# Table transfers behind the first MLP, first operands of the second MLP tile by tile, and one block sum on VectorE: a change in three parts to a two-layer trunk

## The chip, the cores and the metric

The kernel runs on one core of a Trainium2 chip. The metric is the time of one execution on the device in microseconds; a version's time is the median of its runs. A core has five engines, each with its own queue of instructions, which it works off in order: PE (matrix products), DVE (elementwise work on vectors), ACT (activations and copies), POOL (here only transfers, among them those that add to what stands at the target) and SP (here only transfers). Transfers are carried out by 16 DMA engines, which serve the queues of SP and POOL alike.

## The reference

512 tokens of width 1024 pass two layers. Layer 0 mixes by attention, layer 1 by a short gated convolution; after each mixer comes an MLP with a causal convolution of width 3 between its up projection and its gate. All is float32.

```python
def conv_ffn(h, norm_g, w_up, conv_w, w_down):
    xn = rms_norm(h, norm_g)
    u = causal_dwconv(xn @ w_up, conv_w)            # w_up: 1024 x 5632
    g, val = u[..., :D_FF], u[..., D_FF:]           # D_FF = 2816
    return (jax.nn.silu(g) * val) @ w_down

for layer in range(2):
    mixer = attention_mixer if layer % 2 == 0 else short_conv_mixer
    h = h + mixer(h, ...)
    h = h + conv_ffn(h, ffn_norm[layer], ffn_w_up[layer], ffn_conv[layer], ffn_w_down[layer])
```

## The kernel before

Every float32 product is made of three products of rounded halves: an operand is split into `hi` (a rounded copy, made by ACT, named `whi`, `p_hi`, `q_hi`) and `lo` (the rest, made by DVE from the operand and its `hi`, named `wlo`, `p_lo`, `q_lo`), and PE multiplies hi by hi, lo by hi and hi by lo. The helper `halves_to` (L1027, L1029) does this for the operands of the products below, L315 and L316 do it for the weights of the other products. In the trace PE's wait for a weight is therefore a wait for ACT's `whi` or, some 1.2 us later, for DVE's `wlo`.

The up projections go by groups of 256 columns of `w_up` (11 in each MLP, 0 to 10), and each group, but for the first two of the first MLP, by seven products of half-size blocks instead of eight (a Strassen-like scheme, class `Sevens`). The products, in PE's order, are p1, p7, p6, p2, q5, q4 and p3. Each has 24 matmuls (L1078), a form of the activations (made once, before group 0, from blocks a, b, c, d of the normed h; class `RawForms` in the second MLP) and a form of the weights (made for each group). The weights' blocks come into tiles X, Y, Z, W, three and four: some straight from `w_up`, some from tables in DRAM that hold sums of two or three blocks of `w_up`. Where a sum is not in a table, POOL adds a block by an accumulating transfer (`add_block`, L1105). In the second MLP q4's weights are `three` + W, and the sum is made in place in `three`, by such a transfer from `w_up`, after p6's `wlo` has read `three`; the reader of the sum is `whi_q` (`whi_q<-three` in the trace).

The tables (`t` in the trace) are built by POOL's transfers while other work runs (`table_steps`, L104 to L118): a step copies a block or a table (L117) or adds a block (L114), 1 MB or 768 KB each, and a step that builds on another waits for it. Those of the second MLP are 24 steps: 8 before the first MLP (`FAR`), 9 in the first MLP's up loop, one after every seventh slot, and 7 in the conv mixer. POOL takes its queue in order, so a step that waits also holds what stands behind it.

The down projection of an MLP (`mlp()`, L1675) follows after the last group. Its weights X_chain, Y_chain, p_hi_chain and so on (block sums again, the `_chain` tiles are loaded by SP at L291, and POOL adds to them at L289) and `raw` come 512 KB at a time. Where PE goes from the up to the down projection, the last group's products and the first weights of the down projection are wanted at the same time; that place is called the boundary. In the conv mixer, weights come as `raw` for its plain products and as Xc, Yc, Zc and Wc for its seven-product part; POOL adds to Yc at L1105.

The order on an engine is set by a scheduler with estimated times, and within stretches by the program's own order: between the last output tile of the conv mixer's output projection (o == 7) and slot 6 of the second MLP's group 0 the flag `strict` pins ACT and DVE to program order (those instructions have line L74 in the trace). In that stretch, the rest of h arrives, the norm's sum ends in a column `ncol_n` that PE spreads (L396) and ACT copies to `nrow_n`, and the forms p6, p2, q5, q4 of the activations are finished. `Norm.finish(EARLY, LATER)` gives the due times of the spread. s0 and s1 are scratch tiles in which forms that are differences are made.

Of the kernel before, what the change touches and what calls it, by code (L numbers as in the profile page):

```python
# [17 lines left out]
F32 = mybir.dt.float32  # L18
# [4 lines left out]
ALU = mybir.AluOpType  # L23
# [24 lines left out]
FILL1, FILL2, BEFORE = 1.5, 3.3, 2.0  # L48
UNITS = (0, 1), (2,), (3,)
PLAIN = 2, 0  # L50
FAR = 8
CHUNKS = ((2, 3), (5, 3), (8, 3)), ((0, 3), (3, 4), (7, 4))
EARLY, LATER = 4.0, 4.0
SHARE = 0.58


# [1 line left out]
def trunk(  # L58
# [1024 lines left out]
    class Sevens:  # L1083
# [74 lines left out]
        def slot(self, g, s):  # L1158

            on, was, soon = (i in self.groups for i in (g, g - 1, g + 1))  # L1160
            if self.chores:
                self.work_off(self.rate(g, s))
            form, n, fresh = (("p1", "A", True), ("p7", "T", True), ("p3", "R", False), ("p6", "R", False), ("p2", "A", False),
                              ("q5", "R", False), ("q4", "T", False))[s]
            if s == 2:
                if was:
                    self.product(g - 1, form, n, fresh)
            elif on:
                self.product(g, form, n, fresh)
            st, p, c = self.st, g - 1, self.st.get(g)  # L1170
            if s == 0:
                if was:
                    if "p3" not in st[p]:
                        self.weights_of(p, "p3", "Z")
                    self.join(p, "yg", st[p]["T"], st[p]["Xs"])
                if on:
                    self.load_one(g, "W", self.block_of(g, 1, 0))
                if soon:
                    self.load_pair(g + 1)
            elif s == 1:  # L1180
                first = not was
                if on and first and not self.ahead and "p6" not in c:
                    self.weights_of(g, "p6", "three" if self.table else "Y")
                if on:
                    act.activation(self.bank_of(g, "R"), c["A"], AF.Copy, scale=-1.0)
                if on and not first:
                    self.weights_of(g, "p6", "three" if self.table else "Y")
                if soon and not self.table:
                    self.add_block(g + 1, "Y", 1, 1)
            elif s == 2:  # L1190
                if on:
                    self.kept(g, "P7s", c["T"])
                    if "p2" not in c:
                        self.weights_of(g, "p2", "W")
                    if self.fours:
                        self.load_one(g, "four", self.table("4", g))
                    else:
                        c["four"] = c["three" if self.table else "Y"]
                        if self.scaled:
                            self.add_block(g, "four", 1, 0)  # L1200
                        else:
                            dve.tensor_tensor(c["four"], c["four"], c["W"], op=ALU.add)
            elif s == 3:
                if was:
                    self.early(p, st[p]["R"])
# [88 lines left out]
    class RawForms:  # L1294
# [1 line left out]


        def __init__(self, up, x, s0, s1):
            self.up, self.x, self.s = up, x, {"s0": s0, "s1": s1}

        def take(self, f):
            act.activation(self.x[f // 4][:, f % 4, :], h[:, f, :], AF.Copy, scale=gain_of(self.up.norm.base, f))

        def make(self, name, k=slice(0, 4)):
            (a, b), (c, d) = ((x[:, k, LEFT], x[:, k, RIGHT]) for x in self.x)
            s = {n: t() [:, k, :] if callable(t) else t[:, k, :] for n, t in self.s.items() if n == ("s1" if name == "q5" else "s0")}
            src, made = {
                "p1": (a, None), "p7": (s.get("s0"), (a, b, ALU.subtract)), "p6": (s.get("s0"), (s.get("s0"), d, ALU.add)), "p2": (c, None),
                "q5": (s.get("s1"), (b, d, ALU.subtract)), "q4": (d, None), "p3": (s.get("s0"), (c, s.get("s0"), ALU.subtract))}[name]
# [202 lines left out]
    def mlp(layer, norm, mp, begun_up=None):  # L1512
# [63 lines left out]
        n_up = 7 * (HF - PLAIN[layer])  # L1576
        for i, fn in enumerate(slots[:n_up]):
            fn()
            if layer == 0 and i % 7 == 6:
                sum_far(1)  # L1580
            left = n_up - i
            if left <= 2:
                operand(2 - left)
                fetch(3 - left)
# [118 lines left out]
                    finish(b)  # L1703
        if after_:
            after_.finish()
        return after_

    with tc.tile_pool(name="mlp0", bufs=1, reuse_waits="tile") as mp:
# [6 lines left out]
    with tc.tile_pool(name="mlp1", bufs=1, reuse_waits="tile") as mp:  # L1715
        norm = Norm("n3", 8)
        blocks, up = up_begin(1, norm, mp, rp)
        s0 = mp.tile([P, 4, HT], F32, tag="s0", name="s0_up")
        fresh = []

        def s1():
            if not fresh:
                fresh.append(hsp.tile([P, 4, HT], F32, tag="hs_b", name="s1_up"))
            return fresh[0]
        raw = RawForms(up, (place(4, 4), place(8, 4)), s0, s1)

        def out_products(w, acc, ks):
# [4 lines left out]
        def residual_out(o, acc):  # L1732
            dve.tensor_tensor(h[:, o, :], acc, h[:, o, :], op=ALU.add)
            raw.take(o)
            if o == ND - 1:
                raw.make("p6", slice(2, 4))
            norm.squares(o, h[:, o, :])

        first_two = [(weights(AHEAD - o), bank("ab"[o])) for o in range(2)]
# [7 lines left out]
        for o in range(2, ND):  # L1747
# [16 lines left out]

        def slot(g, s):
            up.slot(g, s)
# [29 lines left out]
```

## Time and profile before

| | |
|---|---|
| median of 3 runs | 1134.41 us (1133.47 to 1135.1) |
| the profiled execution | 1134.63 us, span 1132.9 us |
| busy | PE 1115.0, PEld 1016.2, DVE 957.7, ACT 679.8, POOL 175.9 us |
| DMA | 221.42 MB, mean 195 GB/s |
| POOL's queue | 43.4% of 16 engines' span, SP's 34.2% |

The profile counts times from the span's start. The first MLP runs from about 280 to 616 us, with its boundary at 495 to 516; the conv mixer to about 787; the second MLP from there, with its boundary at 1003 to 1016. POOL runs ahead: its last addition for the first MLP is issued at 563.74. A row of a timeline gives the start, the duration, the engine, the line, the operation, the written tile, `<-` and the read ones, and in brackets the idle time of the engine before it with the instruction that ended this. A row of windows gives the busy time of PE, PEld, DVE, ACT and POOL (with the number of instructions), then the granted clock of PE (1.00 is full), the DMA engines' busy share and GB/s. A row of waits gives who waited for whom: total us, times, longest. A row of the chain gives start, duration and what ran.

### The profile page before, as it was taken

How to read it: one execution, taken by the hardware profiler on the slowest of the kernel's cores; microseconds unless marked ns; L12 is line 12 of the kernel's file. 1: busy time of each engine (PE TensorE's matmuls, PEld its weight loads, DVE VectorE, ACT ScalarE, POOL GpSimd, SP SyncE). 2: the span in 40 equal slices, each digit the busy share in tenths (PEclk: the TensorE clock that was granted, in tenths of full speed). 3: DMA queues.
4: the chain of work that ended last, by engine and by line, in shares of the span. 5: the costliest groups of instructions: out<-in, count | busy, mean ns of one | idle time of the engine just before them, and what ended most of it. 6: DMA issues, size and time to landing. Idle time of an engine off the chain costs nothing.

```text
span 1132.9 us, 19709 instructions
## 1 busy us (share of the span) xinstructions
PE 1115.0 (98%) x7803; PEld 1016.2 (90%) x7803; DVE 957.7 (85%) x1471; ACT 679.8 (60%) x999; POOL 175.9 (16%) x204
## 2 busy tenths in 40 slices
PE   9999999999999999989999999999899999989998
PEld 7888787878899999989999899988899999988886
DVE  6798888988898787869989889856899999979886
ACT  7556677655567666656557345545656666557553
POOL 4011011111111120104300001001112121113300
PEclk9999999999999999999999999999999999989999
DMA  6678677777988899899953456697679797799961
GB/s 193 168 179 205 157 196 188 184 208 200 236 205 228 241 251 255 241 320 222 226 166 93 129 133 142 140 273 208 146 189 215 178 218 187 198 286 168 235 156 56
DMA packets 180540, 221.42 MB, mean 195 GB/s; under 512 B 7804, under 2 KB 144044, under 8 KB 180448
## 3 DMA queue, kind: packets, MB, share of 16 engines
q0 software_dynamic: 48912, 97.96, 43.4%
q1 hardware_dynamic: 131376, 122.14, 34.2%
q8 instruction: 61, 1.00, 0.3%
q14 instruction: 31, 0.25, 0.1%
q10 hardware_dynamic: 160, 0.07, 0.0%
HBM read 215.16 MB, written 53.48 MB: 237 GB/s over the span
## 4 chain that ended last, share of the span: by engine, by line
PE 90%; DVE 4%; DMA 3%; ACT 1%; issue 1%; SPq 0%; DVEq 0%; ACTq 0%
PE psb L1078 28%; PE psb L1675 11%; PE psa L1078 10%; PE psa L1675 8%; PE psb L336 6%; PE psb L338 5%; PE psb L337 5%; PE psb L710 2%; PE psa L338 2%; PE psa L337 2%; PE psa L336 2%; PE psa L807 2%; DMA four<-t 1%; DMA three<-in_ffn_w_up 1%; PE psc L782 1%; DMA X_chain<-in_ffn_w_down 1%
## 5 line engine op out<-in xcount | busy, mean ns | idle before, releaser
L1078 PE MATMUL psb<-p_hi,wlo_p 128*128 128x256 f32 x480 | 135.0, 282 | 1.5 <-DVE wlo_p L74 1.5
L1078 PE MATMUL psb<-p_hi,whi_p 128*128 128x256 f32 x480 | 135.1, 282 | 0.0
L1078 PE MATMUL psb<-p_lo,whi_p 128*128 128x256 f32 x480 | 135.1, 282 | 0.0
L315 ACT ACTIVATE whi<-raw 128x1024 fp32r<-128x1024 f32 (+2 forms) x81 | 83.2, 1028 | 81.8 <-PE psb L337 28.0
L316 DVE TENSOR_TENSOR wlo<-raw,whi 128x1024 fp32r<-128x1024 f32 (+2 forms) x81 | 95.7, 1182 | 24.7 <-ACT whi L315 24.1
L1078 PE MATMUL psb<-q_hi,whi_q 128*128 128x256 f32 x320 | 91.1, 285 | 2.7 <-ACT whi_q L1027 2.7
L1078 PE MATMUL psb<-q_hi,wlo_q 128*128 128x256 f32 x320 | 91.5, 286 | 1.9 <-DVE wlo_q L1029 1.9
L1078 PEld LDWEIGHTS psb<-p_hi,wlo_p 128*128 128x128 f32 x480 | 90.1, 188 | 1.7 <-DVE wlo_p L74 1.7
L1078 PE MATMUL psb<-q_lo,whi_q 128*128 128x256 f32 x320 | 91.1, 285 | 0.0
L1078 PEld LDWEIGHTS psb<-p_hi,whi_p 128*128 128x128 f32 x480 | 91.0, 190 | 0.0
L1078 PEld LDWEIGHTS psb<-p_lo,whi_p 128*128 128x128 f32 x480 | 90.4, 188 | 0.0
L1078 PE MATMUL psa<-p_hi,wlo_p 128*128 128x256 f32 x320 | 90.3, 282 | 0.0
L1078 PE MATMUL psa<-p_lo,whi_p 128*128 128x256 f32 x320 | 90.1, 282 | 0.0
L1078 PE MATMUL psa<-p_hi,whi_p 128*128 128x256 f32 x320 | 89.9, 281 | 0.0
L336 PE MATMUL psb<-hs_a,whi 128*128 128x512 f32 x192 | 79.4, 413 | 0.0
L338 PE MATMUL psb<-hs_a,wlo 128*128 128x512 f32 x192 | 76.2, 398 | 0.0
L1078 PEld LDWEIGHTS psb<-q_hi,whi_q 128*128 128x128 f32 x320 | 61.6, 193 | 3.2 <-ACT whi_q L1027 3.1
L1078 PEld LDWEIGHTS psb<-q_hi,wlo_q 128*128 128x128 f32 x320 | 61.2, 191 | 2.6 <-DVE wlo_q L1029 2.6
L1675 PE MATMUL psb<-act,whi 128*128 128x256 f32 x352 | 63.0, 282 | 0.1
L1078 PEld LDWEIGHTS psb<-q_lo,whi_q 128*128 128x128 f32 x320 | 61.3, 191 | 0.0
L1078 PEld LDWEIGHTS psa<-p_hi,whi_p 128*128 128x128 f32 x320 | 60.6, 190 | 0.1
L1078 PEld LDWEIGHTS psa<-p_hi,wlo_p 128*128 128x128 f32 x320 | 60.1, 188 | 0.2 <-DVE wlo_p L1029 0.2
(548 smaller groups left out, 3597.6 us busy)
## 6 DMA issues: line engine op xcount, KB each, us to landing
t<-in_ffn_w_up POOLq DMA_DIRECT2D x30, 768.0 KB, 8.0
raw<-in_attn_w_in SPq DMA_DIRECT2D x24, 512.0 KB, 5.2
t<-in_ffn_w_up POOLq DMA_DIRECT2D x12, 1024.0 KB, 12.6
t<-t POOLq DMA_DIRECT2D x14, 768.0 KB, 4.6
X<-in_ffn_w_up SPq DMA_DIRECT2D x20, 512.0 KB, 5.1
Y<-t SPq DMA_DIRECT2D x20, 512.0 KB, 6.6
three<-t SPq DMA_DIRECT2D x20, 512.0 KB, 5.7
W<-in_ffn_w_up SPq DMA_DIRECT2D x20, 512.0 KB, 4.0
```

Source lines behind the costliest of these rows:

```text
L315: return (act.activation(hi[:, at_], raw[:, at_], AF.Copy), dve.tensor_tensor(lo[:, at_], raw[:, at_], f32(hi[:, at_]), op=ALU.subtract))
L316: dve.tensor_tensor(lo[:, at_], raw[:, at_], f32(hi[:, at_]), op=ALU.subtract))
L336: made = [pe.matmul(acc, w[0], rhs[0], start=first, stop=False), pe.matmul(acc, w[0], rhs[1], start=False, stop=False), pe.matmul(acc, w[1 ...
L337: pe.matmul(acc, w[0], rhs[1], start=False, stop=False),
L338: pe.matmul(acc, w[1], rhs[0], start=False, stop=last)]
L710: pe.matmul(ss[e][:, c:c + wide], ql[rows, b * P:n], kl[rows, 0:wide], start=first and b == bs[0], stop=last and b == bs[-1])
L782: pe.transpose(t[:, k * P:(k + 1) * P], w[:, e, k * P:(k + 1) * P], ident)
L807: pe.matmul(out_, w, t[:, first:first + step * (NB - k - 1) + 1:step, :], start=k == 0 and i == 0, stop=k == NB - 1 and i == 1)
L1078: pe.matmul(to, w[a][:, k, c], x[b][:, k, :], start=fresh and i + k + t == 0, stop=i == 1 and k == 3 and t == 2, skip_group_check=not fresh)
L1675: pe.matmul(to, l, r, start=begin and o + t == 0, stop=end and t == 2 and o == (0 if layer else 1), skip_group_check=not fresh)
```

## The change

Three parts.

1. The 9 table steps of the first MLP's up loop are issued after the first MLP's last instructions (`sum_far(BETWEEN)` behind `after_.finish()`).
2. In the last group of the second MLP, where no group follows (`soon` is false), the sum `three` + W is made by DVE from the W that is loaded anyway, and not by POOL's transfer.
3. In the second MLP, the forms p6, p2, q5 and q4 are made for tiles 0 and 1 after output tile 5, for tile 2 after tile 6, and for tile 3 after tile 7; before, p6 was made in two halves and the others whole, late. s1 is taken from the two buffers of X instead of from `hs_b`, which comes free only late. `LATER` goes from 4.0 to 5.0.

```diff
-FAR = 8
+FAR, BETWEEN = 8, 9
-EARLY, LATER = 4.0, 4.0
+EARLY, LATER = 4.0, 5.0
...
                         c["four"] = c["three" if self.table else "Y"]
-                        if self.scaled:
+                        if self.scaled and soon:
                             self.add_block(g, "four", 1, 0)
                         else:
                             dve.tensor_tensor(c["four"], c["four"], c["W"], op=ALU.add)
...
         for i, fn in enumerate(slots[:n_up]):
             fn()
-            if layer == 0 and i % 7 == 6:
-                sum_far(1)
...
         if after_:
             after_.finish()
+            sum_far(BETWEEN)
...
-        def s1():
-            if not fresh:
-                fresh.append(hsp.tile([P, 4, HT], F32, tag="hs_b", name="s1_up"))
-            return fresh[0]
+        s0, s1 = mp.tile([P, 4, HT], F32, tag="s0", name="s0_up"), mp.tile([P, 4, HT], F32, tag="X", name="s1_up", bufs=2)
...
             if o == ND - 1:
-                raw.make("p6", slice(2, 4))
+                raw.make("p6", slice(3, 4))
...
             elif o == 5:
-                raw.make("p6", slice(0, 2))
+                for n in ("p6", "p2", "q5", "q4"):
+                    raw.make(n, slice(0, 2))
             elif o == 6:
                 up.weights_of(0, "p1", "X")
+                raw.make("p6", slice(2, 3))
                 up.first_sums(0)
+                for n in ("p2", "q5", "q4"):
+                    raw.make(n, slice(2, 3))
         norm.finish(EARLY, LATER)
-        more = {0: lambda: up.weights_of(0, "p6", "three"), 1: lambda: (up.weights_of(0, "p2", "W"), raw.make("p2")), 2: lambda: raw.make("q5"),
-                3: lambda: raw.make("q4"), 5: lambda: raw.make("p3"), 6: lambda: strict.__setitem__(0, False)}
+        late = slice(3, 4)
+        more = {0: lambda: up.weights_of(0, "p6", "three"), 1: lambda: (up.weights_of(0, "p2", "W"), raw.make("p2", late)),
+                2: lambda: (raw.make("q5", late), raw.make("q4", late)), 5: lambda: raw.make("p3"), 6: lambda: strict.__setitem__(0, False)}
```

On POOL, the end of the first MLP's up loop before the change, with the table steps between the additions to the groups' X (L1105) and ahead of the down projection's additions (L289):

```order
L117 DMA t_3276<-in_ffn_w_up 256x1024
L1105 DMA X_5026<-in_ffn_w_up 128x4x256
L114 DMA t_3276<-in_ffn_w_up 256x1024
L1105 DMA X_5267<-in_ffn_w_up 128x4x256
L117 DMA t_3279<-t_3276 256x1024
L1105 DMA X_5508<-in_ffn_w_up 128x4x256
L114 DMA t_3279<-in_ffn_w_up 256x1024
L117 DMA t_3277<-in_ffn_w_up 256x1024
L289 DMA p_hi_chain_0_6126<-in_ffn_w_down 128x2x512
```

And with the change, at the end of the down projection's additions, ahead of the conv mixer's Yc:

```order
L289 DMA q_lo_chain_0_6300<-in_ffn_w_down 128x2x512
L117 DMA t_3276<-in_ffn_w_up 256x1024
L114 DMA t_3276<-in_ffn_w_up 256x1024
L117 DMA t_3279<-t_3276 256x1024
L114 DMA t_3279<-in_ffn_w_up 256x1024
L117 DMA t_3276<-in_ffn_w_up 256x1024
L114 DMA t_3276<-in_ffn_w_up 256x1024
L117 DMA t_3279<-t_3276 256x1024
L114 DMA t_3279<-in_ffn_w_up 256x1024
L117 DMA t_3277<-in_ffn_w_up 256x1024
L1105 DMA Yc_7654<-in_conv_w_in 128x4x256
```

All nine have moved past the down projection's 24 additions on the same queue.

On DVE, at the start of the second MLP before the change, from the last output tile's h on (8668 to 8673 are the halves of p6, p2 and q5; `s_up` is s0 in the first two of its rows and s1 in the others):

```order
L74 TENSOR_TENSOR h<-psb_8944,h 128x512
L74 TENSOR_TENSOR s_up<-s_up,hs_a_conv 128x512
L74 TENSOR_TENSOR p_lo_8669<-s_up,p_hi_8668 128x512
L74 TENSOR_TENSOR nacc_n_8661<-nacc_n_8661,sq_n_8974 128x512
L74 TENSOR_TENSOR wlo_p_9009<-three_8942,whi_p_9008 128x1024
L74 TENSOR_TENSOR wlo_p_9044<-W_9002,whi_p_9043 128x1024
L74 TENSOR_TENSOR p_lo_8671<-hs_a_conv,p_hi_8670 128x1024
L74 TENSOR_TENSOR s_up<-hs_a_conv 128x1024
L74 TENSOR_TENSOR q_lo_8673<-s_up,q_hi_8672 128x1024
L74 TENSOR_SCALAR nv_n_9063<-psc_9025 128x4
```

And with the change (8674 and 8675 are q4's halves):

```order
L74 TENSOR_TENSOR h<-psb_8962,h 128x512
L74 TENSOR_TENSOR s_up<-s_up,hs_a_conv 128x256
L74 TENSOR_TENSOR p_lo_8669<-s_up,p_hi_8668 128x256
L74 TENSOR_TENSOR nacc_n_8661<-nacc_n_8661,sq_n_8992 128x512
L74 TENSOR_TENSOR wlo_p_9027<-three_8953,whi_p_9026 128x1024
L74 TENSOR_TENSOR wlo_p_9062<-W_9020,whi_p_9061 128x1024
L74 TENSOR_TENSOR p_lo_8671<-hs_a_conv,p_hi_8670 128x256
L74 TENSOR_TENSOR s_up<-hs_a_conv 128x256
L74 TENSOR_TENSOR q_lo_8673<-s_up,q_hi_8672 128x256
L74 TENSOR_TENSOR q_lo_8675<-hs_a_conv,q_hi_8674 128x256
L74 TENSOR_SCALAR nv_n_9082<-psc_9043 128x4
```

The late pieces are a quarter as wide, and q4's now stands before the norm's first step `nv_n`, whose last step makes `ncol_n`; the other pieces have moved ahead of the h of the first row.

On PE, at the same place with the change, from p2's last matmul on (psb_9059 takes q5, psb_9030 takes q4):

```order
L1078 MATMUL psa_8995<-p_hi_8670,wlo_p_9062 128x256
L1078 MATMUL psb_9059<-q_hi_8672,whi_q_9126 128x256
L1078 MATMUL psb_9059<-q_lo_8673,whi_q_9126 128x256
L396 MATMUL psc_9164<-ident,ncol_n_9084 128x128 x4
L1078 MATMUL psb_9030<-q_hi_8674,whi_q_9156 128x256
L1078 MATMUL psb_9030<-q_lo_8675,whi_q_9156 128x256
L1078 MATMUL psb_9059<-q_hi_8672,wlo_q_9127 128x256
```

Before, the spread of `ncol_n` stood right behind p2, followed by eight transposes of h, all 24 matmuls of q5 and then those of q4. Now two matmuls of q5 stand ahead of the spread, the transposes come later, and the first two of q4 stand ahead of the other 22 of q5. On SP, the order of the transfers is the same, but X of group 1 goes to the buffer that s1 leaves.

On DVE, in the last group of the second MLP with the change:

```order
L1029 TENSOR_TENSOR wlo_p_11475<-three_11409,whi_p_11474 128x1024
L446 SCALAR_TENSOR_TENSOR ug_11370<-y_both_11372,taps,ug_11370 128x510
L1202 TENSOR_TENSOR three_11409<-three_11409,W_11442 128x1024
L1029 TENSOR_TENSOR wlo_p_11508<-W_11442,whi_p_11507 128x1024
L1127 TENSOR_TENSOR y_both_11372<-psb_11236,nrow_n_9163 128x2x256
```

The third row is new; one row of POOL (`L1105 DMA three<-in_ffn_w_up`) is gone, and the rest of DVE's order there is the same.

More of the change, by code (lines that the diff above doesn't have):

```diff
@@ L1298, in __init__ @@
         def __init__(self, up, x, s0, s1):
-            self.up, self.x, self.s = up, x, {"s0": s0, "s1": s1}
+            self.up, self.x, self.s = up, x, (s0, s1)
         def take(self, f):
@@ L1305, in make @@
             (a, b), (c, d) = ((x[:, k, LEFT], x[:, k, RIGHT]) for x in self.x)
-            s = {n: t() [:, k, :] if callable(t) else t[:, k, :] for n, t in self.s.items() if n == ("s1" if name == "q5" else "s0")}
+            s0, s1 = (t[:, k, :] for t in self.s)
             src, made = {
-                "p1": (a, None), "p7": (s.get("s0"), (a, b, ALU.subtract)), "p6": (s.get("s0"), (s.get("s0"), d, ALU.add)), "p2": (c, None),
-                "q5": (s.get("s1"), (b, d, ALU.subtract)), "q4": (d, None), "p3": (s.get("s0"), (c, s.get("s0"), ALU.subtract))}[name]
+                "p1": (a, None), "p7": (s0, (a, b, ALU.subtract)), "p6": (s0, (s0, d, ALU.add)), "p2": (c, None),
+                "q5": (s1, (b, d, ALU.subtract)), "q4": (d, None), "p3": (s0, (c, s0, ALU.subtract))}[name]
             if made:
@@ L1717, in trunk @@
         blocks, up = up_begin(1, norm, mp, rp)
-        s0 = mp.tile([P, 4, HT], F32, tag="s0", name="s0_up")
-        fresh = []
-        def s1():
-            if not fresh:
-                fresh.append(hsp.tile([P, 4, HT], F32, tag="hs_b", name="s1_up"))
-            return fresh[0]
+        s0, s1 = mp.tile([P, 4, HT], F32, tag="s0", name="s0_up"), mp.tile([P, 4, HT], F32, tag="X", name="s1_up", bufs=2)
         raw = RawForms(up, (place(4, 4), place(8, 4)), s0, s1)
```

## The prediction

> **What bounds the kernel now.** I read the page's table of busy time, then the waits on PE, then the chain of waits and the timelines at the places that those name.
>
> ```profile
> PE 1115.0 (98%) x7803; PEld 1016.2 (90%) x7803; DVE 957.7 (85%) x1471; ACT 679.8 (60%) x999; POOL 175.9 (16%) x204
> PE psb L1078 <- ACT whi_q L1027: 2.7, 2, 2.5
> PE psb L1078 <- DVE wlo_q L1029: 1.9, 3, 0.8
> PE psc L396 <- DVE ncol_n L74: 1.5, 1, 1.5
> PE psb L1078 <- DVE wlo_p L74: 1.5, 1, 1.5
> PE psa L1675 <- DVE wlo L316: 1.5, 2, 0.8
> PE psa L1675 <- ACT whi L315: 1.2, 1, 1.2
> PE psc L1596 <- ACT nrow_n L74: 0.3, 1, 0.3
> ```
>
> PE is busy 98% of the span and the change removes no matmul, so it can win only PE's waits (total us, times, longest) and stretches of slow matmuls. The sum is made against the profiled execution's 1134.63 us, 0.2 above the median of 1134.41. About 0.2%, 2.3 us, is what a measurement can tell from no change.
>
> **Part 2, the last group's four-block sum on DVE.** The chain and PE's timeline in group 10 of the second MLP, and two stretches:
>
> ```profile
> 995.40 12.34 DMA three<-in_ffn_w_up
> 1006.16 0.28 PE L1078 MATMUL psb<-q_hi,wlo_q 128*128 128x256 f32 x1
> 1008.93 0.39 PE L1078 MATMUL psb<-q_hi,whi_q 128*128 128x256 f32 x1 [2.49 <-ACT whi_q L1027]
> 1010.20 0.58 PE L1078 MATMUL psb<-q_hi,wlo_q 128*128 128x256 f32 x1 [0.66 <-DVE wlo_q L1029]
> 1015.05 0.63 PE L1675 MATMUL psa<-whi,act 128*128 128x512 f32 x1
> ...
> 1000.00:1005.00 5.00, 5.00 (x45) 5.00 (x44) 3.40 (x6) 1.25 (x3) 1.84 (x2) 1.00 1.11 298
> 1010.00:1015.00 5.00, 4.80 (x22) 4.81 (x23) 5.00 (x8) 2.12 (x4) 0.00 (x0) 0.50 1.09 298
> ```
>
> The accumulating transfer takes 12.34 us, `whi_q` and `wlo_q` of product q4 follow it, and PE waits 2.49 and 0.66. Then the granted clock (last column but two) is 0.50: 22 matmuls in 5 us instead of 45. Without the transfer q4's 24 matmuls would follow that of 1006.16 at 5/45 = 0.11 to 0.12 us and end near 1009.0, where the down phase (L1675) would begin instead of at 1015.05: 6.0 us, and 0.3 for its first, still slow matmuls. What replaces it is one addition on DVE:
>
> ```profile
> 996.72 1.23 DVE L1029 TENSOR_TENSOR wlo_p<-W,whi_p 128x1024 fp32r<-128x1024 f32 x1 [0.94 <-ACT whi_p L1027]
> 1011.08 1.04 ACT L315 ACTIVATE whi<-X_chain 128x1024 fp32r<-128x1024 f32 x1
> X_chain<-in_ffn_w_down SPq DMA_DIRECT2D x1, 512.0 KB, 10.6
> ```
>
> It has `wlo_p`'s size (1.23) and comes just ahead of it, where DVE idles 0.94: `wlo_p` moves by some 0.3 us, hidden behind p6's matmuls. The sum is there near 998, eight us before PE asks for q4's `whi` at 1006.3 (`whi` takes 1.04, as below, and nothing else of ACT is late there). Late next is the down phase's second operand: X_chain lands at about 1010.75 (10.6 after its issue at 1000.18). PE, six us earlier, needs it after 12 matmuls of 0.23, at 1011.9; its `whi` ends near 1012.1 and its `wlo` 1.2 later. That is a wait of 0 (if the load, with 512 KB less beside it, lands two us sooner) to 1.8; I take 0.9. **Part 2: -5.4** (-6.3 to -3.2, the two waits alone).
>
> **Part 1, nine table steps behind the first MLP.** The last two share the DMA engines with that MLP's last operands (issues of POOL and the chain; the last row is the two steps' time to landing):
>
> ```profile
> 478.10 1.48 POOL L117 DMA_DIRECT2D t<-in_ffn_w_up  x1
> 492.21 10.04 DMA X_chain<-in_ffn_w_down
> 513.19 0.03 ACTq L315
> 513.38 1.05 ACT whi L315
> t<-in_ffn_w_up POOLq DMA_DIRECT2D x2, 1024.0 KB, 14.4
> ```
>
> They fly until about 493. X_chain needs 10.04 us, and its `whi` (1.2 on PE) and `wlo` (0.8) are made right after it lands; before them whi_q 0.2 (2.7 less 2.5) and wlo_q 0.8 wait for a table's block, and near 375 wlo_q another 0.4, beside another step. The second wlo, 0.8, follows a `whi` at 513.38 that PE itself releases (ACT's queue at 513.19): it stays. Gain 0 (if the loads are late for other reasons) to 3.4; I take 3.4, since 2 MB leave the queue and X_chain has to land only 2.5 us sooner.
>
> The cost is where they go: behind POOL's last addition for the first MLP and ahead of Yc's. Below stand rows of the timelines, of the issues by line in three stretches (KB each, median us to landing), and one stretch of the windows.
>
> ```profile
> 599.65 1.28 POOL L1105 DMA_DIRECT2D Yc<-in_conv_w_in  x1 [34.73 <-DMA Yc<-in_conv_w_in]
> 656.37 1.04 ACT L1027 ACTIVATE whi_p7c<-Yc 128x1024 fp32r<-128x1024 f32 x1
> t<-in_ffn_w_up POOLq DMA_DIRECT2D x5, 1024.0 KB, 11.3
> t<-t POOLq DMA_DIRECT2D x2, 1024.0 KB, 6.0
> raw<-in_conv_w_out SPq DMA_DIRECT2D x8, 512.0 KB, 10.6
> ...
> raw<-in_ffn_w_down SPq DMA_DIRECT2D x2, 512.0 KB, 5.1
> 574.65 1.06 ACT L315 ACTIVATE whi<-raw 128x1024 fp32r<-128x1024 f32 x1 [1.69 <-DMA raw<-in_ffn_w_down]
> 580.99 1.06 ACT L315 ACTIVATE whi<-X_chain 128x1024 fp32r<-128x1024 f32 x1 [1.20 <-PE psa L1675]
> 565.00:575.00 10.00, 10.00 (x87) 10.00 (x87) 8.62 (x13) 4.45 (x7) 0.00 (x0) 1.00 1.07 260
> p_hi_chain<-in_ffn_w_down SPq DMA_DIRECT2D x1, 512.0 KB, 15.0
> ```
>
> POOL is free from 599.65 - 34.73 = 564.9. By the conv stage's prices (additions 11.3, copies 6.0) the waits between the nine steps sum to 6 + 11.3 + 6 + 11.3 + 11.3 + 6 = 52 us (a new pair's copy runs beside the addition ahead of it), so Yc's addition is issued near 617 and lands some 6 later, 33 us before `whi_p7c` reads it at 656.37: hidden. In the conv stage loads beside such steps take 10.6 us (raw), against 5.1 for the down phase's last raws, and the DMA share at 565 to 575 is 1.07 already. ACT waits for the raw that it reads at 574.65. PE is done with that operand when it frees the buffer at 580.9, so it begins it 24 matmuls (2.85 us) earlier, at 578.1, where `whi` and `wlo` were ready by about 577: a reserve of 1 to 2 us. Three to five us later it costs 1 to 4 us, less if the loads keep their pace: 0 to 4. I take 1.2, since the first step is a plain copy (6.0). **Part 1: -2.2** (-3.4 to +4).
>
> **Part 3, the second MLP's first operands.** It aims at ncol_n 1.5, nrow_n 0.3 and wlo_p 1.5 (above), 3.3 us.
>
> ```profile
> 566.30 0.42 DVE L1574 TENSOR_TENSOR head_blocks<-head_blocks,hs_a_blocks 128x256 f32<-128x256 f32 x1
> 800.69 0.16 DVE L74 SCALAR_TENSOR_TENSOR ncol_n<-rb_n,ry_n 128x4 f32<-128x4 f32 x1
> 799.09 0.28 PE L1078 MATMUL psa<-p_hi,wlo_p 128*128 128x256 f32 x1
> 792.75 1.29 POOL L1105 DMA_DIRECT2D three<-in_ffn_w_up  x1 [5.63 <-DVE wlo_p L74]
> 800.00:805.00 5.00, 3.84 (x31) 3.54 (x32) 4.33 (x9) 2.98 (x4) 0.00 (x0) 1.00 0.02 5
> three<-in_ffn_w_up POOLq DMA_DIRECT2D x1, 512.0 KB, 7.3
> X<-in_ffn_w_up POOLq DMA_DIRECT2D x1, 512.0 KB, 8.2
> ```
>
> Behind the last h, p2_lo, s1 and q5_lo shrink from 128x1024 (1.23, as `wlo_p` above) to 128x256 (0.42, the first row) each: 2.4 us. The smaller pieces of the other tiles, now ahead of that h, delay it by 1 to 2. ncol_n is ready near 799, when PE has done p2 (799.09): both norm waits go. But q4's first two matmuls now stand before 22 of q5's, so PE asks for q4's `whi` at 799.9. That needs the addition into `three`: issued 0.7 later than 792.75, since `wlo_p` ahead of it is, it takes 7.3 (as before) to 8.2 (the X addition with three loads beside it; here too, for X, Y, Z and `three` of group 1 now queue on SP until s1 is read, near 796). It lands at 800.8 to 801.7, `whi` 1.1 later: a wait of 2.0 to 2.9, say 2.3. It covers the later wlo_p wait, but X of group 1, loaded 26 us later than before, may come late: 0 to 2, say 0.3. **Part 3: -3.3 + 2.6 = -0.7** (-2.5 to +1, to +4 with what follows on the clock).
>
> The clock: after waits of 2.49 and 0.66 it fell to 0.50, after the norm's 1.5 and 0.3 not (1.00 in 800:805); 2.3 lies between. If it falls again, that costs what it cost there, 6.3 - 3.2 = 3.1 us. [...]
>
> **Sum:** -5.4 - 2.2 - 0.7 = -8.3: 1126.3 us.
>
> **Rivals.** (a) The boundary at 495 to 515 is late for its own loads: in the last group, with no table step about, X_chain also takes 10.6. Then part 1 gives 0.4 - 1.2 = +0.8: 1129.3. Against it: there POOL's 12.34 us addition flies beside it, here two steps of twice its bytes. (b) The wait for q4's `whi` at 800 halves the clock: 1126.3 + 3.1 = 1129.4. (c) No new waits: transfers land sooner everywhere, 1134.6 - 6.3 - 3.4 - 3.0 = 1121.9. (d) Slower: the moved steps starve the raws near 570. If they take as long as the slowest load beside two steps (p_hi_chain, 15.0), the one read at 574.65, issued 5.1 before that, lands near 584.5 and its `wlo` is ready 2.3 later: PE waits 8.7 us from 578.1 and the clock halves, 3.1. That is 1134.6 - 5.4 - 3.4 - 0.7 + 11.8 = 1136.9, slower than before; up to 12.7 us for the load it is not. Against it: mostly one step at a time flies there.
>
> **How the numbers follow.** Forecast 0.53, (a) 0.13, (b) 0.16, (c) 0.09, (d) 0.09. The forecast's own range is 1123.5 to 1129, (a) and (b) reach 1131 with their bounds, (c) 1121.5: 1121.5 to 1131 leaves (d) and the tails of (a) and (b) out. Under 1132.1 counts as faster: all but (d) and a tail, 0.90; (d) and the tail split into same 0.05 and slower 0.05.
>
> **What would show it.** Part 2: q4's `whi` of group 10 before PE asks, the clock 1.00 throughout 1000 to 1015 of today's time, the down phase some 6 us sooner and a wait of about 1 for `whi` or `wlo` of X_chain. Part 1: waits at the first MLP's boundary down to the one `wlo`, nine t rows on POOL from 565 to about 620, and a wait for raw's `whi` or `wlo` near 577. Part 3: no wait for ncol_n, one for whi_q behind it. I am wrong if the waits at the boundary stay, if PE stands over 3 us at 577 or 800, or if the clock drops where it did not before.

## The result and the profile after

The changed kernel takes 1122.81 us (median of 4, 1121.57 to 1122.95) against 1134.76 for the kernel before on the same chip (median of 4, 1133.47 to 1136.45): ratio 0.9891, 95% interval 0.9874 to 0.9909, faster by 1.1% or 11.95 us. The forecast was 1126.3, 8.3 us of gain. The time lies inside the stated range of 1121.5 to 1131, but 0.7 us below the forecast's own 1123.5 to 1129, and nearest to rival (c), 1121.9. The profiled execution took 1121.57 us with a span of 1119.8 and a mean granted clock of 1.00.

The page's busy times and PE's waits (total us, times, longest) after, to be read beside the first fence of the prediction:

```profile
PE 1109.3 (99%) x7803; PEld 1011.9 (90%) x7803; DVE 958.8 (86%) x1482; ACT 680.4 (61%) x1006; POOL 174.3 (16%) x203
PE psa L336 <- ACT whi L315: 1.3, 1, 1.3
PE psa L1673 <- DVE act L1031: 1.0, 2, 0.7
PE psb L1078 <- ACT whi_q L74: 0.5, 1, 0.5
PE psb L1673 <- DVE act L1031: 0.4, 1, 0.4
```

All waits that the change aimed at are gone from this execution. The two `act` rows and `whi_q` are new (the line L1673 was L1675 before). The first row stands in the attention stage, which the change leaves alone.

Both kernels run the same 7803 matmuls, so a ledger can be made from PE's timeline: when the k-th matmul starts in each, and how far the changed kernel leads.

```
before's PE time, us      300   370   480   530   650   720   770   820   985  1050   end
lead of changed, us       0.1   0.3   1.6   6.8   4.8   3.5   3.5   6.7   6.7  13.1  13.1
```

The first MLP's up loop and its boundary gain 6.5 (0.3 to 6.8), the first MLP's down phase and the conv stage give 3.3 back, the start of the second MLP gains 3.2, and its last group gains 6.4. The end is the difference of the two profiled executions, 1134.63 - 1121.57 = 13.06. The windows (length, then busy time and count of PE, PEld, DVE, ACT and POOL, clock, DMA share, GB/s) show most of it as idle time of PE, three stretches of before and then the same of after:

```profile
485.00:560.00 75.00, 71.35 (x593) 70.28 (x592) 62.40 (x84) 44.27 (x63) 24.08 (x22) 1.00 1.06 263
560.00:720.00 160.00, 159.90 (x1158) 150.16 (x1157) 140.21 (x176) 88.04 (x113) 11.44 (x9) 1.00 0.53 134
780.00:820.00 40.00, 36.68 (x276) 34.47 (x275) 31.93 (x46) 23.46 (x30) 5.19 (x4) 1.00 0.59 129
```

```profile
485.00:560.00 75.00, 75.00 (x636) 75.00 (x636) 67.45 (x93) 48.39 (x68) 27.22 (x25) 1.00 1.04 239
560.00:720.00 160.00, 157.66 (x1129) 147.20 (x1128) 137.17 (x171) 84.78 (x110) 16.34 (x17) 1.00 0.73 184
780.00:820.00 40.00, 39.49 (x318) 38.40 (x317) 35.09 (x58) 25.97 (x38) 5.16 (x4) 1.00 0.72 172
```

Idle falls from 3.65 to 0 at the boundary, rises from 0.10 to 2.34 where the table steps went (DMA share 0.53 to 0.73), and falls from 3.32 to 0.51 at the second MLP's start. In the last group the clock stays up. The sum is made at 988.88; the first row below is the stretch that leads up to q4's matmuls, which begin near 999.5, and in the second the down phase begins, at 1002.31 (1015.05 before):

```profile
995.00:1000.00 5.00, 5.00 (x45) 5.00 (x44) 5.00 (x8) 3.76 (x6) 2.46 (x2) 1.00 1.00 245
1000.00:1005.00 5.00, 5.00 (x33) 4.53 (x33) 5.00 (x7) 1.70 (x2) 0.00 (x0) 1.00 1.06 245
```

### The profile page after: what moved, and what is told of

It is laid out like the page before. It is cut to its first block, busy times and chain, and to the rows that moved or that the text cites. A ratio compares the mean times of both kernels' runs of the same rounds, so it can differ in the third digit from the quotient of the medians.

```text
span 1119.8 us, 19731 instructions
## 1 busy us (share of the span) xinstructions
PE 1109.3 (99%) x7803; PEld 1011.9 (90%) x7803; DVE 958.8 (86%) x1482; ACT 680.4 (61%) x1006; POOL 174.3 (16%) x203
## 4 chain that ended last, share of the span: by engine, by line
PE 82%; DVE 7%; DMA 5%; issue 3%; ACT 2%; SPq 0%; ACTq 0%; DVEq 0%; POOLq 0%
PE psb L1078 28%; PE psa L1078 11%; PE psb L1673 10%; PE psa L1673 7%; PE psb L336 4%; PE psb L338 4%; PE psb L337 4%; PE psb L710 2%; PE psa L807 2%; DVE wlo L316 1%; DMA Xc<-in_conv_w_in 1%; DMA raw<-in_conv_w_in 1%; DMA raw<-in_conv_w_out 1%; PE psc L782 1%; PE psa L338 1%
## 5 line engine op out<-in xcount | busy, mean ns | idle before, releaser
L1673 PE MATMUL psb<-act,whi 128*128 128x256 f32 x352 | 63.1, 282 | 0.5 <-DVE act L1031 0.4
L1078 PEld LDWEIGHTS psa<-p_lo,whi_p 128*128 128x128 f32 x320 | 60.2, 188 | 0.1
```

The costliest lines, as they stand in the source:

```text
L1078: pe.matmul(to, w[a][:, k, c], x[b][:, k, :], start=fresh and i + k + t == 0, stop=i == 1 and k == 3 and t == 2, skip_group_check=not fresh)
L1673: pe.matmul(to, l, r, start=begin and o + t == 0, stop=end and t == 2 and o == (0 if layer else 1), skip_group_check=not fresh)
```

## The experiments

Times are medians; ranges are over all executions of a kernel, and the clock is the mean granted clock of an execution. Executions of one kernel differ in part by the clock that they were granted. On the first chip used here the kernel before took 1134.0 to 1134.6 us at a clock of 0.998 and 1137 to 1139.6 at 0.992, though two executions at 0.997 also took 1137.3 and 1137.5.

**Each part alone.** On one chip (before 1135.70), the kernel before plus one part. First part 1:

```diff
-FAR = 8
+FAR, BETWEEN = 8, 9
-            if layer == 0 and i % 7 == 6:
-                sum_far(1)
             after_.finish()
+            sum_far(BETWEEN)
```

> Only part 1 (nine table steps behind the first MLP), the rest as before. Theory A (the parts act at separate places and add up, as the two traces read): the waits at 375 and 495 to 516 go, all of them, the second wait for wlo at 516 too, since ACT's whi there stood behind the activation of ug, which waited for a late DVE, and not behind PE: -5.2 us of start-to-start excess; new waits of some 1.9 us at 570 to 592 (raw late) and 1.0 at 660 to 710 (Yc late): net -2 to -3 us. Theory B (the prediction's reading): the second wlo wait of 0.8 stays; gain 3.4, cost 1.2, net -2.2, and nothing new after 600. The two differ in the trace, at 516 and at 660 to 710.

Then part 2:

```diff
-                        if self.scaled:
+                        if self.scaled and soon:
```

> Only part 2 (the last group's sum of four blocks on DVE). Theory A: both waits before q4 go and the clock stays at 1.00, X_chain lands in time because the transfer that is gone had also held it: -6.3 us, no wait after the boundary. Theory B: X_chain takes its 10.6 us and PE waits about 0.9 for its whi or wlo: -5.4 us. Theory C (the half clock at 1009 has another cause than the waits): -3.2 us, and 22 matmuls in 5 us still stand there.

And part 3, the pieces by tile, s1's place and `LATER`:

```diff
-EARLY, LATER = 4.0, 4.0
+EARLY, LATER = 4.0, 5.0
...
-                raw.make("p6", slice(2, 4))
+                raw.make("p6", slice(3, 4))
...
```

> Only part 3 (first operands of the second MLP tile by tile). Theory A: the waits for ncol_n, nrow_n and wlo_p (3.8 us of excess with their small followers) go and a wait of 0.7 for q4's whi comes: -3 us, the accumulating transfer into three takes under 6 us since the loads of group 1 are issued three us after it. Theory B: that transfer is late or slow, a wait of 2.3 for q4's whi: -0.7 us, or, if the clock then halves, +2.

Measured: part 1 alone 1133.14 (1130.2 to 1146.47), ratio 0.9993 [0.9968, 1.0018]; part 2 alone 1130.04 (1127.95 to 1132.32), 0.9958 [0.9944, 0.9971]; part 3 alone 1135.44 (1130.87 to 1137.08), 0.9991 [0.9978, 1.0004]. The three ratios add up to 0.6% and the whole change is worth 1.1%; by the medians the parts are worth 2.6, 5.7 and 0.3 us.

At a like clock it comes out better: at 0.998 part 1 alone takes 1130.2 to 1131.0 against 1134.0 to 1134.6, so 3.6 to 3.8 less (3.2 in the ledger), and part 3 at 0.997 to 0.998 takes 1130.9 to 1132.5, 2.1 less between the medians of those executions (3.2). Executions picked by their clock after the fact are weak evidence. The traces are better: the ledger made in the same way for each part's own trace shows the gain in its place, 5.2 at 480 to 530 with part 1 alone, 6.3 in the last group with part 2 alone and 2.2 at the second MLP's start with part 3 alone. Part 1's trace has no wait left at 375 and from 495 to 516, and part 2's none behind the second boundary, as Theory A says of both. So each mechanism is there alone; what is lost again is lost elsewhere.

The three traces keep PE waits of 1.8 to 4.1 us. Behind the longest the clock halves in the traces of parts 1 and 3, and behind 1.8 in that of part 2 it does not. PE's waits in the last group and its windows there, with part 1 alone and then with part 3 alone:

```profile
PE psb L1078 <- ACT whi_q L1027: 3.0, 1, 3.0
1005.00:1010.00 5.00, 3.67 (x20) 3.47 (x21) 4.46 (x6) 3.75 (x6) 0.00 (x0) 0.78 1.11 252
```

```profile
PE psb L1078 <- ACT whi_q L1027: 4.5, 2, 4.1
1010.00:1015.00 5.00, 2.98 (x12) 2.68 (x13) 3.46 (x5) 4.30 (x6) 0.00 (x0) 0.52 1.12 224
1015.00:1020.00 5.00, 5.00 (x26) 4.50 (x26) 5.00 (x7) 1.06 (x1) 0.00 (x0) 0.79 0.94 314
```

The wait for POOL's sum is not a constant: 2.49 before, 3.0 and 4.1 here. The kernel with part 2 removes it, and with it one of the places where the other parts' gains are lost. It is not the only one: part 3's trace loses 1.0 us against before in the last group, but also 1.7 in a stretch of half clock near 60 (0.79 in 55:60, 0.87 in 60:65), in the attention stage, which the change leaves alone, and 1.8 between 820 and 985.

**One part undone.** On another chip (before 1136.12), from the changed kernel without part 1 (the first diff above, reversed), and without part 3:

> The changed kernel with part 1 undone (table steps in the first MLP's up loop). Theory A (the parts add up while the clock stays at 1.00): 2.5 to 4 us slower than the changed kernel, the waits of 3 to 4.5 back at 495 to 516 and those at 570 to 710 gone. Theory B (what a part leaves of waits also drops the clock): two groups of executions, the slower by some 1.7 us for each spell of half clock of 3.4 us, so 4 to 6 us slower than the changed kernel by the median.

> The changed kernel with part 3 undone (first operands of the second MLP as before). Theory A: the waits of 1.7, 0.45 and 1.7 at 796 to 809 are back, 3.8 less the 0.7 for q4's whi: 3 us slower than the changed kernel, the clock at 1.00 there. Theory B: a spell of half clock as well in some executions, 3 to 5 us.

Measured: without part 1 1127.65 (1124.52 to 1128.16), 0.9917 [0.9898, 0.9937]; without part 3 1126.45 (1123.97 to 1127.14), 0.9909 [0.989, 0.9927]; the changed kernel itself on that chip, run again:

> The changed kernel once more, to stand on one chip with the next three. Theory A (its executions differ by where loads land): most near 0.989 of the kernel before, clock 0.998 to 1.00; now and then an execution some 10 us longer, in which the conv mixer's raw near 617, beside two table steps and Yc's addition, lands after some 16 us and PE waits about 8. Theory B (no such rare executions): all within 2 us.

1124.53 (1122.92 to 1134.87), 0.9912 [0.988, 0.9945]. By medians part 1 is worth 3.1 and part 3 1.9, but the intervals overlap: two of the changed kernel's six executions took 1129.32 and 1134.87. The profiles show what the times leave open. From 300 to 720 us the ledger's lead grows by 0.2 without part 1 and by 3.4 with it, and from 790 to 820 by 0.0 without part 3 and by 3.2 with it. Without part 3 the waits for `ncol_n` and `wlo_p` are back at 1.5 each, word for word as in before's rows; without part 1 those of the first boundary are, the one for `wlo` at 1.5 again and, of these two rows, the second whole and 0.4 of the first (waits of PE):

```profile
PE psb L1078 <- DVE wlo_q L1029: 1.3, 3, 0.8
PE psa L1675 <- ACT whi L315: 1.3, 1, 1.3
```

No stretch of the two profiles shows a lower clock until the last few microseconds: in these two executions, with part 2 in, the waits cost what they last and no more. Other executions of the two kernels had a mean clock of 0.997 or 0.998, and where they lost it was not traced.

**Where the table steps stand.** Part 1's 3.3 us of cost should depend on the place. All nine behind Yc's addition, in the conv stage:

```diff
                 up.add_block(1, "Y", 1, 1)
+                sum_far(BETWEEN)
...
-            sum_far(BETWEEN)
```

> The changed kernel with the nine table steps issued one place later on POOL, behind the conv mixer's first addition to Yc. Theory A: part 1's cost is the collision with the last raws of the down phase (570 to 592) and with Yc's addition (15 us to land): both go, 1.5 to 2.7 us faster than the changed kernel, some -13.5 to -14.5 from before. Theory B: the steps only collide with other loads, the conv mixer's raws at 610 to 626 and the Xc addition behind them at 660: new waits of 1 to 4 us there, as fast as the changed kernel or slower.

Measured: 1124.88 (1123.65 to 1126.3), 0.9907 [0.9894, 0.992], no faster than changed. The waits of 570 to 592 are gone, but a 1.1 us wait for `wlo_p1c` (657) has come, with two of 0.3 behind it that the changed kernel has too: much the same traffic, met by other operands. (A wait of 0.8 for `nacc_n` at 789 comes as well, but one of 0.9 stands there with part 3 alone and one of 0.4 without part 1, both with the steps in the up loop, so it is not shown to be the steps' doing.) Neither of the two places took all nine steps without new waits. Six were put back into the up loop, and three behind Yc:

```diff
-FAR, BETWEEN = 8, 9
+FAR, BETWEEN = 8, 3
                 up.add_block(1, "Y", 1, 1)
+                sum_far(BETWEEN)
...
+            if layer == 0 and i % 7 == 6 and i < 42:
+                sum_far(1)
...
-            sum_far(BETWEEN)
```

> The changed kernel with six of the nine table steps back in the first MLP's up loop (one after every seventh slot, up to the sixth) and the last three behind the conv mixer's first addition to Yc. Theory A (the boundary at 495 is hurt by the steps that are in flight there alone, and the moved steps cost by colliding with the last raws and by holding Yc): no wait at 495 to 516, about 0.8 back at 375, none at 570 to 592, less than 0.5 at 660 to 710: 1 to 2 us faster than the changed kernel. Theory B (the load on the DMA engines in the whole up loop makes the boundary late): waits of 2 us or more come back at 495 to 516, and it is slower than the changed kernel.

> Six table steps in the first MLP's up loop and three behind Yc's addition, beside the changed kernel on one chip. Theory A: no waits at 570 to 592 and 660 to 670, no second step beside Yc's addition: 0.5 to 2 us faster than the changed kernel, and no execution 10 us longer. Theory B: as fast as the changed kernel.

Measured: 1122.20 (1120.02 to 1124.79), 0.9879 [0.9859, 0.99], and on the chip of the changed kernel's second run 1122.29 (1121.65 to 1125.29), 0.988 [0.9859, 0.9901], 2.2 us under its 1124.53. Windows of the first:

```profile
485.00:560.00 75.00, 75.00 (x634) 75.00 (x633) 67.19 (x90) 47.31 (x67) 26.48 (x24) 1.00 1.03 238
560.00:720.00 160.00, 159.44 (x1151) 149.68 (x1151) 139.47 (x175) 86.68 (x111) 13.39 (x12) 1.00 0.57 146
```

With six steps in the loop the boundary stays free, as Theory A has it: the last two of before's nine, which flew near it, are gone. The idle time behind it is 0.56 instead of 2.34. None of its 11 executions was a long one. It beats the kernel before beyond doubt and the changed kernel by its medians on both chips; the intervals overlap, so that second claim is not proven.

**The due time.** `LATER` back to 4.0 in the changed kernel, to part the smaller pieces from the norm's due time:

```diff
-EARLY, LATER = 4.0, 5.0
+EARLY, LATER = 4.0, 4.0
```

> The changed kernel with LATER back at 4.0. In the program's order the norm's spread then stands ahead of p2's last matmul, eight transposes follow, and all of q5 stands ahead of q4. Theory A (the late pieces' size took the norm's wait away, and q4 ahead of q5 costs the 0.7 us that the trace shows): the wait for q4's whi goes, a wait of 0 to 0.6 for ncol_n may come; within 1 us of the changed kernel. Theory B (the later due time is what took the norm's wait away): the wait of 1.5 for ncol_n comes back, 1 to 2 us slower than the changed kernel.

Measured: 1125.71 (1123.41 to 1128.44), 0.9909 [0.989, 0.9929]. PE's rows:

```profile
799.06 1.38 PE L1594 MATMUL psc<-ident,h 128*128 128x128 f32 x8
811.06 0.38 PE L1078 MATMUL psb<-p_hi,wlo_p 128*128 128x256 f32 x1 [1.52 <-DVE wlo_p L74]
```

The wait for `ncol_n` stays away, so that one is removed by the smaller pieces alone. But the wait of 1.5 for `wlo_p` is back: the eight transposes of h now run early, and at 5.0 seven of them run (805.89) just ahead of the place where PE would have waited. That was in neither theory.

**How much lateness the last group bears.** Idle ACT work of four, then five activations was put ahead of q4's `whi` in the changed kernel's last group (their results are not used):

```diff
+                    if self.scaled and not soon:
+                        for _ in range(4):
+                            pin(act.activation(self.spare, c["four"], AF.Copy))
...
+        up.spare = s0
```

> The changed kernel with four idle activations of 128x1024 on ACT (their results are not used) ahead of q4's whi in the last group, so that PE waits for it by about 1.6 us and for wlo by another 0.7. Theory A (the clock falls when PE stands for about 2.5 us or more in a stretch, as before the change): clock 1.00 throughout, 2.5 to 3 us slower than the changed kernel. Theory B (whether the clock falls is not set by the wait's length alone): some executions of this kernel have a clock under 1.00 and take 3 us more than others.

> The same with five idle activations: waits of about 2.6 and 0.7, as before the change, but without the transfer that caused them. Theory A: the clock falls in every execution, 3.3 us for the waits and 3.1 for the clock, 6.4 slower than the changed kernel. Theory B: executions of both kinds, some 3.3 and some 6.4 slower. If the clock never falls, it was not the wait but something of the transfer.

Measured: 1127.24 (1125.71 to 1137.15), 0.9918 [0.9894, 0.9941], and 1130.66 (1127.96 to 1132.67), 0.9951 [0.9936, 0.9967]. By the medians the fifth activation, about 1 us of work (`whi_q`, of the same size, takes 1.05 in after), costs 3.4. All five executions with four have a mean clock of 0.993 to 0.998 and all seven with five one of 0.995 to 0.998, so the clock fell somewhere in each, which Theory A had wrong for four. PE's rows and a window with four, then with five:

```profile
1012.77 0.38 PE L1078 MATMUL psb<-q_hi,whi_q 128*128 128x256 f32 x1 [1.36 <-ACT whi_q L1027]
1013.72 0.73 PE L1676 MATMUL psa<-whi,act 128*128 128x512 f32 x2 [0.45 <-ACT whi L315]
1015.00:1020.00 5.00, 5.00 (x26) 4.72 (x25) 2.67 (x5) 1.06 (x1) 0.16 (x1) 0.69 0.79 271
```

```profile
1006.61 0.39 PE L1078 MATMUL psb<-q_hi,whi_q 128*128 128x256 f32 x1 [2.45 <-ACT whi_q L1027]
1005.00:1010.00 5.00, 2.95 (x13) 2.62 (x14) 4.06 (x4) 3.45 (x4) 0.00 (x0) 0.81 1.09 281
```

Even 1.36 and 0.45 were followed by half clock in this execution. Against the changed kernel's ledger the last group loses 3.9 in the first trace and 5.0 in the second, only 1.1 apart, so the 3.4 between the medians is not the price of one activation. Both traces also have a stretch of half clock at 575 to 580 (0.73 and 0.70), behind waits of 0.73 and 0.96 and of 0.85 and 0.96 for the first MLP's last operands; the changed kernel's profile has 0.70 and 0.33 there and a clock of 1.00. The execution with four was also the long one, for another reason, in the chain of waits:

```profile
617.30 16.06 DMA raw<-in_conv_w_in
633.45 1.06 ACT whi L315
634.53 1.22 DVE wlo L316
PE psc L396 <- DVE ncol_n L434: 8.0, 1, 8.0
```

A raw weight of the conv stage lands after 16.06 us beside the last table steps and Yc's addition (issued at 617.23 and 617.79), and PE stands 8 us (last row, from PE's waits). That is rival (d)'s mechanism, 50 us later than where it was looked for. The same raw, the second of five, took 6.4 in the changed kernel's profile, where the two steps and the addition came 3.6 us later (620.31 to 621.44); the fourth and fifth took 13.8 and 12.9 there without a wait. In the two profiles of the six-and-three kernel PE stands for 0.07 us at most between 600 and 660. A late raw is the likely cause of the changed kernel's 1134.87 and of part 1's 1146.47 as well; those executions were not traced, so this is argued, not shown.

## Why the prediction was right, and where its terms were off

**Part 2 (-5.4 predicted, 6.4 gained).** The sum, q4's readiness, the clock at 1.00 and the earlier down phase came as worked out. The term that failed is the 0.9 for X_chain's `whi` and `wlo`: it was taken as a middle of 0 to 1.8, and is 0. Rows of after, from DVE's timeline, ACT's timeline and the issues (KB, us to landing):

```profile
988.88 1.22 DVE L1202 TENSOR_TENSOR three<-three,W 128x1024 f32<-128x1024 f32 x1
994.89 1.05 ACT L1027 ACTIVATE whi_q<-three 128x1024 fp32r<-128x1024 f32 x1
X_chain<-in_ffn_w_down SPq DMA_DIRECT2D x1, 512.0 KB, 6.1
```

The load took 6.1, not 10.6: without POOL's transfer beside it, it landed 4.5 us sooner, where 2 had been allowed for.

**Part 1 (-2.2 predicted; 6.5 gained, 3.3 given back, net 3.2).** Its net is 1 us off, but both terms were too small. The gain: rival (a) fell, as X_chain landed in 4.1 instead of 10.0. The whole boundary is PE alone in the chain of waits after (fourth and last of its seven pieces from 485 to 520), and the step that failed is that the second `wlo`, 0.8, stays:

```profile
496.21 8.52 PE psa L1673 x72
...
514.67 5.44 PE psb L1673 x46
X_chain<-in_ffn_w_down SPq DMA_DIRECT2D x1, 512.0 KB, 4.1
```

I read its `whi` at 513.38 as released by PE, from the chain. The timelines of DVE and ACT say otherwise, of before and then of after:

```profile
503.44 1.22 DVE L316 TENSOR_TENSOR wlo<-X_chain,whi 128x1024 fp32r<-128x1024 f32 x1 [2.90 <-ACT whi L315]
512.41 1.06 ACT L1285 ACTIVATE ug<-ug 128x1024 f32<-128x1024 f32 x1 [2.60 <-DVE ug L446]
513.38 1.04 ACT L315 ACTIVATE whi<-p_hi_chain 128x1024 fp32r<-128x1024 f32 x1
```

```profile
504.51 1.06 ACT L1285 ACTIVATE ug<-ug 128x1024 f32<-128x1024 f32 x1 [1.48 <-DVE ug L446]
505.48 1.04 ACT L315 ACTIVATE whi<-p_hi_chain 128x1024 fp32r<-128x1024 f32 x1
```

`whi` stood behind `ug` on ACT's queue, and `ug` behind DVE, which had lost 2.90 us to X_chain at 503.44 and then worked without a gap until `ug`'s input: one late load, felt twice. With the load in time DVE does not wait there, and `whi` is made at 505.48, before PE needs it at 507.57. The ledger has 1.3 of the gain between 370 and 480, 1.0 of it near 375 (0.4 was counted there, without what PE loses around a wait), and 5.2 at 480 to 530.

The cost: predicted 0 to 4, taken 1.2, measured 3.3. The place was right. Rows of after: the second of the two raws in the chain of waits, ACT's reads of both, PE's first wait, and the first table step (POOL's timeline and the issues):

```profile
564.02 8.58 DMA raw<-in_ffn_w_down
569.29 1.06 ACT L315 ACTIVATE whi<-raw 128x1024 fp32r<-128x1024 f32 x1 [3.07 <-DMA raw<-in_ffn_w_down]
572.71 1.06 ACT L315 ACTIVATE whi<-raw 128x1024 fp32r<-128x1024 f32 x1 [1.84 <-DMA raw<-in_ffn_w_down]
572.27 0.39 PE L1673 MATMUL psa<-act,whi 128*128 128x256 f32 x1 [0.70 <-DVE act L1031]
557.68 1.09 POOL L117 DMA_DIRECT2D t<-in_ffn_w_up  x1
t<-in_ffn_w_up POOLq DMA_DIRECT2D x1, 1024.0 KB, 14.5
```

PE's row names `act`, but `act` stands behind `wlo<-raw` on DVE, and that behind the raw. With the lead of 6.8 taken off, ACT reads the first raw 1.4 us later than before (569.29 against 574.65), and PE waits 0.70 for it; the second, which took 8.58 against 5.1, is read 2.8 later (before at 576.74), and PE waits another 0.33.

The term that was mis-sized is the first step. It was taken as a plain copy of 6.0, but 6.0 is the row of `t<-t`; this step copies from `w_up`, and the one such copy of before's conv stage took 13.7. Here it took 14.5 and flew until 572.17, beside both raws. (In rival (d) the raw read at 574.65 was put 5.1 after its issue; it was issued at 567.88, 6.8 before, and 5.1 belongs to the next one.) 1.6 us go this way, and 0.4 at 592, where DVE is still late.

Yc's addition was issued at 621.44, not near 617, and took 15.1, not 6; it stayed hidden all the same. The other 1.35, at 663 to 710, came from conv operands that no step of the sum looked at: in the conv stage the reserve was checked for Yc only, and not for the other operands.

**Part 3 (-0.7 predicted, 3.2 gained).** The waits that it aimed at, 3.3 us, went whole. The term that failed is the price behind it: 2.3 for q4's `whi` and 0.3 for X were 0.5 and 0. From DVE's and PE's timelines and the issues:

```profile
795.32 0.16 DVE L74 SCALAR_TENSOR_TENSOR ncol_n<-rb_n,ry_n 128x4 f32<-128x4 f32 x1
796.99 0.39 PE L1078 MATMUL psb<-q_hi,whi_q 128*128 128x256 f32 x1 [0.51 <-ACT whi_q L74]
805.89 0.93 PE L1594 MATMUL psc<-ident,h 128*128 128x128 f32 x7
three<-in_ffn_w_up POOLq DMA_DIRECT2D x1, 512.0 KB, 5.8
```

The addition into `three` took 5.8, not 7.3 to 8.2; group 1's loads, which were to fly beside it, were issued 2.8 us and more behind it. It was issued 0.8 later by PE's time, as had been worked out (790.08 with the lead of 3.5 is 793.6). So rival (b) had no wait of 2.3 to work with. That such a wait leaves the clock alone, as the sum has it, no run shows: with part 2 alone the clock stayed at 1.00 after waits of 1.82 and 0.76, with part 3 alone it fell after 2.12 and 0.76 (0.66 in 505:510). The wait for `wlo_p` was to be covered by q4's wait; it is covered by the transposes in the third row instead, as the run with the due time of 4.0 showed.

In all, four waits were priced too dear (X_chain's, the second `wlo`, q4's `whi`, X's) and one cost too cheap. Two of the dear ones have one source: X_chain and `three` were priced at about what they took before, though the change itself removes or moves what flew beside them. The cost has the same source the other way round: the raws slowed down beside what the change puts there. (X of group 1 did slow down, from 8.2 to 9.95, but it landed at 810.49, before ACT read it at 812.16.) PE's idle time in the traces of all runs bears this out. At the first boundary (495 to 520) PE stood 2.9 to 3.7 us in the four with all nine steps in the up loop and 0.00 in the ten others. In the last group, where 0.9 had been set down for X_chain, it stood 0.15 at most from 1000 to 1015 in the nine traces with part 2 and no added activations. q4's `whi` at the second MLP's start kept PE 0.5 to 0.9 us in the lists of waits with part 3 (not at all with the due time of 4.0), never 2.3.

Rival (c) came nearest in time by the sum of these errors and not by its mechanism: there were new waits, which cost 3.3 us behind part 1 and 0.5 at q4's `whi`. That the time lies in the stated range is in part luck, since it reached down to 1121.5 only to take in (c).

## What to carry to other kernels

Price a transfer by what will fly beside it after the change, not by its row of before: 512 KB took about 4 to 16 us here (4.1 for X_chain at the first boundary after, 16.06 for a raw of the conv stage with four added activations). Before you call a late operand the fault of another engine, read what stands ahead of it on its own engine's queue; one late load may be behind two waits (here X_chain's, of 10.04 us, behind PE's 1.2 for `whi` and, by the 2.90 that DVE lost, behind its 0.8 for the second `wlo`). Try to spread moved transfers over several covers instead of putting all behind one (here that won by the medians only), and time a change of several parts as a whole as well as in parts, since a wait that is left in can hand the other parts' gain back through the clock (with part 1 alone 0.78 and 0.88 in the two stretches from 1005, behind 3.0 and 0.8).

## What the runs showed of the hardware

The clock after a wait was the surprise. It fell to half after PE waits of 2.49 and 0.66 us (before), 3.0 and 0.8 (part 1 alone), 4.1 and 0.5 (part 3 alone), 2.45 and 0.45 (five activations), and 1.36 and 0.45 (four); with part 3 alone also at the first boundary, after the wait in the first row below and one of 0.76. In the two kernels with activations it fell after 0.73 and 0.96 and after 0.85 and 0.96 as well (near 574). In the part 3 and the due-time kernels it fell near 58 (0.79 in 55:60 of both), behind a wait of 0.6 for `w` that stands there in before and after too (0.55 at 56.74 and at 56.66) and left the clock at 1.00 in these. It did not fall after nearly the same pair as in the first row in the part 2 kernel (third and fourth row, clock 1.00 there), nor after the norm's 1.5 and 0.3:

```profile
504.19 0.50 PE L1675 MATMUL psa<-act,whi 128*128 128x256 f32 x2 [2.12 <-ACT whi L315]
505.00:510.00 5.00, 4.55 (x27) 4.55 (x28) 5.00 (x8) 3.25 (x6) 0.00 (x0) 0.66 1.10 274
```

```profile
502.00 0.50 PE L1675 MATMUL psa<-act,whi 128*128 128x256 f32 x2 [1.82 <-ACT whi L315]
503.26 0.39 PE L1675 MATMUL psa<-act,wlo 128*128 128x256 f32 x1 [0.76 <-DVE wlo L316]
```

A half-clock spell lasted about 3.4 us (5 x (1 - 0.66) x 2 in the second row) or twice that (6.9 with part 3 alone in the last group: 5 x 0.48 x 2 + 5 x 0.21 x 2), if the clock within it is the 0.50 that before's row at 1010 shows. So a wait's length alone does not decide: the pair at the first boundary cost its own length with part 2 alone and 1.7 us more with part 3 alone (half of a spell of 3.4), and 4.1 and 0.5 in the last group cost 3.4 more (half of 6.9). 1.36 and 0.45 us were enough for half clock in one execution, and 0.73 and 0.96 in another stretch of it, while 1.82 and 0.76 were not in the part 2 kernel's. What decides beside the length no run here settles.
